# Strassen sums of a SwiGLU feed-forward kept in PSUM, gate and up products interleaved, weight sums formed by accumulating loads

## The chip, the cores and the metric

One core of a Trainium2 chip runs the whole kernel in one launch. The metric is device time in microseconds, and the result is the median of several runs. The engines are TensorE (PE, with its weight loads listed as PEld), VectorE (DVE), ScalarE (ACT), GpSimd (POOL) and SyncE (SP, which here only starts transfers).

## The reference

Two layers of a trunk of width 1024 over 512 latent tokens and 256 context tokens. Each layer is a feed-forward, a mixer of four head groups, and a second feed-forward. The feed-forwards are what the change touches:

```python
def swiglu(h, w_gate, w_up, w_down):
    return (jax.nn.silu(h @ w_gate) * (h @ w_up)) @ w_down

h_lat = h_lat + 0.5 * m_l[2] * swiglu(modulate(rms_norm(h_lat, g_ffn1[l]), m_l[0], m_l[1]),
                                      w1_gate[l], w1_up[l], w1_down[l])
```

All data are fp32, `D_FF` is 2816. Three of the four feed-forwards run over 768 tokens; the last layer's second one runs over the 512 latent tokens alone.

## The kernel before

Every fp32 operand is split into a rounded part `hi` and a rest `lo` (ACT copies `hi` at L143, DVE subtracts at L144), and a matmul of fp32 numbers is three matmuls in PE's float32r format, `lo·hi + hi·lo + hi·hi` (`mm3`, L172). All matmuls of the feed-forward have line L172.

A feed-forward (`ffn`, L504) works through the 2816 hidden channels in six chunks of 4, 2, 4, 4, 4, 4 blocks of 128. The first chunk is done by `first_pairs`. Each of the others is done two blocks at a time by `gate_up` (nine calls in a feed-forward, 36 in the kernel), and then `down` multiplies the chunk's result `g` by `w_down` and adds it to the residual `h` (L306).

`gate_up` computes, for the gate matrix (`m` = 0) and then for the up matrix (`m` = 1), a 2 x 2 block product by Strassen's method in Winograd's form: seven products in place of eight. The weights are four 128 x 512 pieces a11, a12 (first block of channels) and a21, a22 (second block); the tokens are two halves of `hn` columns (384, in the last feed-forward 256), whose seven combinations (B11, B21, T1 and so on) are made once per feed-forward by `token_sums`. One product is four times `mm3`, 12 matmuls of `hn` columns into one PSUM bank. The order of the products is 1, 2, 5, 6, 7, 4, 3. Four of the seven need sums of weights (`ws`, DVE, L454 and L460 in the trace): a21+a22, then minus a11, a11-a21, and a12 minus the second. The products are added to each other by DVE out of PSUM (`tt`, same lines), with one copy by ACT (L478). `ready` takes a finished quarter: SiLU on ACT for the gate (L450), for up the multiplication on DVE and the split into `g`.

`unit` splits a 128 x 512 piece of weights into a pair of tiles from the ring `wr`. That ring has five pairs, and `N_WX` more in a feed-forward: six in all over 768 tokens, ten over 512. A pair comes free when the 12 matmuls that read it are done. `load` takes the next of four `raw` tiles (128 x 1024) in turn and starts the transfer on SP's queue. SP issues in order, and waits in order for tiles to come free.

PSUM has eight banks: six `ps`, and `pone` and `pmod`, which are lent to the feed-forward as banks except where `fills` still needs `pmod` for the modulation vectors (`mod_group`, L189).

The program's order on each engine comes from a list scheduler at compile time. It goes by the order in which the code issues and by a model of durations; `rise(n)` moves what is inside it ahead by `n` places. On the chip each engine runs its list strictly in order.

Of the kernel before, what the change touches and what calls it, by code (L numbers as in the profile page):

```python
# [11 lines left out]
AF = mybir.ActivationFunctionType  # L12
ALU = mybir.AluOpType
AX = mybir.AxisListType

P = 128
# [30 lines left out]
class K:  # L47
# [114 lines left out]
        self.nc.sync.dma_start(r[:parts, :width], src)  # L162
        return r

    def mm3(self, ps, w, x, start, stop):

        (wh, wl), (xh, xl) = w, x
        n = xh.shape[-1]
        for i, (a, b) in enumerate(((wl, xh), (wh, xl), (wh, xh))):
            for c in range(0, n, 512):  # L170
                e = min(n, c + 512)
                self.nc.tensor.matmul(ps[:, c:e], a, b[:, c:e], start=start and i == 0, stop=stop and i == 2)  # L172


    def mod_group(self, l, blocks):
# [132 lines left out]

    def token_operands(self, X, hn, r, gain, l, part, half, kk):

        hi, lo = X[(("B11", "B21"), ("B12", "B22"))[half][kk]]
        for k in range(4):
            s = slice(k * hn, (k + 1) * hn)
            t = self.tmp.popleft()[:, :hn]
            self.modulated(hi[:, s], lo[:, s], t, 4 * kk + k, r, gain, l, part, half * hn, (half + 1) * hn)
            self.tmp.append(t)

    def token_sums(self, X, hn):  # L320

        tt = self.nc.vector.tensor_tensor
        for k in range(4):
            s = slice(k * hn, (k + 1) * hn)
            (b11, c11), (b21, c21), (b12, c12), (b22, c22) = (
                (X[n][0][:, s].bitcast(F32), X[n][1][:, s].bitcast(F32)) for n in ("B11", "B21", "B12", "B22"))
            t, u = (self.tmp.popleft()[:, :hn] for _ in range(2))
            out = lambda n, x: self.split(X[n][0][:, s], X[n][1][:, s], x)
            tt(out=t, in0=b12, in1=b11, op=ALU.subtract)
            tt(out=u, in0=c12, in1=c11, op=ALU.subtract)  # L330
            tt(out=t, in0=t, in1=u, op=ALU.add)
            out("T1", t)
            tt(out=t, in0=b22, in1=t, op=ALU.subtract)
            tt(out=t, in0=t, in1=c22, op=ALU.add)
            out("T2", t)
            tt(out=u, in0=b22, in1=b12, op=ALU.subtract)
            tt(out=t, in0=t, in1=b21, op=ALU.subtract)
            tt(out=t, in0=t, in1=c21, op=ALU.subtract)
            v = self.tmp.popleft()[:, :hn]
            tt(out=v, in0=c22, in1=c12, op=ALU.subtract)  # L340
# [44 lines left out]
    def first_pairs(self, idx, X, g, hn, norm, operands, fills, start):  # L385
# [45 lines left out]
        for f in range(2, 4):  # L431
            self.plain(idx, f, X, g[f], hn, fills)

    def gate_up(self, idx, f, X, g, hn, fills):

        nc = self.nc
        T, SW = self.tmp.popleft, self.sw
        mats = [{}, {}]
        act = {}

        def prod(ps, w, name):
            xh, xl = X[name]
            for k in range(4):
                self.mm3(ps, (w[0][:, k * P:(k + 1) * P], w[1][:, k * P:(k + 1) * P]),
                         (xh[:, k * hn:(k + 1) * hn], xl[:, k * hn:(k + 1) * hn]), k == 0, k == 3)

        def ready(m, i, j, c):

            if m == 0:
                nc.scalar.activation(c, c, AF.Silu)  # L450
                act[i, j] = c
            else:
                t = act[i, j]
                nc.vector.tensor_tensor(out=t, in0=c, in1=t, op=ALU.mult)  # L454
                s = slice(j * hn, (j + 1) * hn)
                self.split(g[i][0][:, s], g[i][1][:, s], t)
                self.tmp.extend((t, c))

        def tt(eng, out, p, q, op):
            eng.tensor_tensor(out=out, in0=p, in1=q, op=op)  # L460
            return out

        def ws(out, p, q, op):
            return tt(vec, out, p, q, op)

        vec = nc.vector
        for m, M in enumerate(mats):
            self.spot(fills)
            for step in (1, 2, 5, 6, 7, 4, 3):
                if step == 1:  # L470
                    M["r"] = [self.load(self.a["w_gu"][idx, f + j, :, m, :], 1024) for j in range(2)]
                (a11, a12), (a21, a22) = ((r[:, :512], r[:, 512:]) for r in M["r"])
                bank = self.banks.popleft()
                ps = bank[:, :hn]
                if step == 1:
                    prod(ps, self.unit(a11), "B11")
                    M["p1"] = T()[:, :hn]
                    nc.scalar.activation(M["p1"], ps, AF.Copy)  # L478
                elif step == 2:
                    prod(ps, self.unit(a12), "B21")  # L480
                    ready(m, 0, 0, tt(vec, T()[:, :hn], M["p1"], ps, ALU.add))
                elif step == 5:
                    M["s"] = ws(SW[0], a21, a22, ALU.add)
                    prod(ps, self.unit(M["s"]), "T1")
                    M["p5"], bank = bank, None
                elif step == 6:
                    prod(ps, self.unit(ws(M["s"], M["s"], a11, ALU.subtract)), "T2")
                    M["u2"] = tt(vec, M["p1"], M["p1"], ps, ALU.add)
                elif step == 7:
                    prod(ps, self.unit(ws(SW[1], a11, a21, ALU.subtract)), "T3")  # L490
                    M["u3"] = tt(vec, T()[:, :hn], M["u2"], ps, ALU.add)
                    tt(vec, M["u2"], M["u2"], M["p5"][:, :hn], ALU.add)
                elif step == 4:
                    prod(ps, self.unit(a22), "T4")
                    ready(m, 1, 0, tt(vec, T()[:, :hn], M["u3"], ps, ALU.subtract))
                    ready(m, 1, 1, tt(vec, M["u3"], M["u3"], M["p5"][:, :hn], ALU.add))
                    self.banks.append(M["p5"])
                elif step == 3:
                    prod(ps, self.unit(ws(M["s"], a12, M["s"], ALU.subtract)), "B22")
                    ready(m, 0, 1, tt(vec, M["u2"], M["u2"], ps, ALU.add))  # L500
                if bank is not None:
                    self.banks.append(bank)

    def ffn(self, l, which, part, n, cuts, fills, start=None):  # L504

# [2 lines left out]
        idx = l * 2 + which  # L508
        hn = n // 2
        with ExitStack() as st:  # L510
            tmp = st.enter_context(self.area("t"))
# [17 lines left out]
            for ci, nf in enumerate(F_CHUNKS):  # L529
# [891 lines left out]
```

## Time and profile before

| what | value |
|---|---|
| median of 3 runs | 2690.11 us (2685.78 to 2691.51) |
| the profiled execution, its own time | 2696.05 us |
| its span from first to last instruction | 2694.2 us |
| PE busy | 2629.0 us (98%), 16021 matmuls |
| DVE busy | 2005.3 us (74%) |
| ACT busy | 1133.1 us (42%) |
| POOL busy | 76.6 us (3%) |
| transfers | 254.15 MB, mean 94 GB/s; every transfer of the program on SP's queue |

Busy is the share of the span in which at least one instruction of the engine was in flight. Matmuls overlap their neighbours, so a matmul's own duration is longer than the time from its start to the next one's start; the latter is what sets the pace.

### The profile page before, as it was taken

To read this page: it belongs to the slowest core of one execution; us is meant where nothing else is said; L and a number is where in the kernel's file an instruction comes from. 1 tells how busy PE (TensorE), PEld (TensorE's weight loads), DVE (VectorE), ACT (ScalarE), POOL (GpSimd) and SP (SyncE) were. 2 spreads that over 40 slices of the span, in tenths; PEclk is the share of its full clock that TensorE was granted. 3 is DMA by queue.
4 is the path that set the end of the run, shared out by engine and by line. 5 is a ranking of instruction groups with operands and counts; after the bars stand their busy time and mean duration, and the time that the engine had idled before them with its cause. 6 is when DMAs were issued, how large, how long until landed. Compare 5 with 4: busy or idle time off the path is not lost.

```text
span 2694.2 us, 40622 instructions
## 1 busy us (share of the span) xinstructions
PE 2629.0 (98%) x16021; PEld 2450.3 (91%) x16021; DVE 2005.3 (74%) x3888; ACT 1133.1 (42%) x2125; POOL 76.6 (3%) x98
## 2 busy tenths in 40 slices
PE   7999999999999999999999999999999999999998
PEld 5999999988887999999999999999998776889998
DVE  5777667679967476767667868677679985788887
ACT  4323323343567342334324523343334576544444
POOL 0000000000212000000000000000000111000000
PEclk9999999999989999999999999999999999999999
DMA  7323223221134342223223112221222133423322
GB/s 257 124 78 119 86 79 110 94 71 50 38 110 145 128 137 96 95 86 118 92 81 122 43 55 63 71 79 56 74 75 80 35 118 119 134 84 103 95 95 79
DMA packets 78272, 254.15 MB, mean 94 GB/s; under 512 B 8704, under 2 KB 14336, under 8 KB 77824
## 3 DMA queue, kind: packets, MB, share of 16 engines
q1 hardware_dynamic: 78080, 251.56, 28.9%
q8 instruction: 125, 2.05, 0.3%
q14 instruction: 67, 0.55, 0.1%
HBM read 249.43 MB, written 2.10 MB: 93 GB/s over the span
## 4 chain that ended last, share of the span: by engine, by line
PE 86%; DVE 8%; ACT 2%; DMA 2%; issue 1%; POOL 0%; SPq 0%; DVEq 0%; ACTq 0%; POOLq 0%
PE ps L172 66%; PE pone L172 8%; PE pmod L172 5%; PE pmod L189 3%; DVE f L631 2%; DMA raw<-in_w_gu 1%; PE ps L606 1%; DVE wl L144 1%; PE pone L770 1%; DVE r L144 1%; PE pone L771 0%; DVE f L144 0%; DMA raw<-in_w_mod 0%; DVE sm L885 0%; DVE sm L833 0%
## 5 line engine op out<-in xcount | busy, mean ns | idle before, releaser
L172 PE MATMUL ps<-x,wh 128*128 128x384 f32 (+1 forms) x3064 | 748.6, 329 | 0.0
L172 PEld LDWEIGHTS ps<-x,wh 128*128 128x128 f32 x3064 | 542.9, 188 | 0.1
L172 PE MATMUL ps<-x,wl 128*128 128x384 f32 (+1 forms) x1532 | 505.1, 330 | 0.0
L143 ACT ACTIVATE wh<-raw 128x512 fp32r<-128x512 f32 (+1 forms) x439 | 275.0, 628 | 435.6 <-PE ps L172 268.5
L144 DVE TENSOR_TENSOR wl<-raw,wh 128x512 fp32r<-128x512 f32 (+1 forms) x439 | 303.1, 692 | 115.7 <-ACT wh L143 113.5
L172 PE MATMUL ps<-t,wh 128*128 128x384 f32 (+2 forms) x1488 | 385.8, 341 | 0.3 <-DVE t L144 0.3
L306 DVE SCALAR_TENSOR_TENSOR h<-ps,hg,h 128x256 f32<-128x256 f32 (+3 forms) x404 | 186.7, 506 | 183.0 <-PE ps L172 182.5
L172 PEld LDWEIGHTS ps<-x,wl 128*128 128x128 f32 x1532 | 287.7, 188 | 7.5 <-issue 3.7
L143 ACT ACTIVATE wh<-t 128x512 fp32r<-128x512 f32 x217 | 136.4, 631 | 337.7 <-PE ps L172 199.6
L172 PEld LDWEIGHTS ps<-t,wh 128*128 128x128 f32 x1488 | 269.2, 188 | 7.1 <-DVE t L144 0.5
L172 PE MATMUL ps<-r,wh 128*128 128x512 f32 (+3 forms) x1070 | 260.9, 335 | 0.6 <-DVE r L301 0.5
L460 DVE TENSOR_TENSOR t<-t,ps 128x384 f32<-128x384 f32 (+1 forms) x422 | 217.6, 521 | 51.7 <-PE ps L172 49.5
L172 PE MATMUL ps<-t,wl 128*128 128x384 f32 (+2 forms) x744 | 253.0, 341 | 2.0 <-ACT t L143 2.0
L143 ACT ACTIVATE t<-t 128x384 fp32r<-128x384 f32 (+2 forms) x247 | 130.7, 537 | 212.3 <-DVE t L454 101.8
L144 DVE TENSOR_TENSOR wl<-t,wh 128x512 fp32r<-128x512 f32 x217 | 149.3, 690 | 92.2 <-ACT wh L143 92.0
L172 PE MATMUL ps<-x,t 128*128 128x384 f32 (+1 forms) x1308 | 204.2, 309 | 0.0
L172 PEld LDWEIGHTS ps<-r,wh 128*128 128x128 f32 (+1 forms) x1070 | 180.3, 188 | 22.3 <-DVE r L301 1.7
L172 PEld LDWEIGHTS ps<-x,t 128*128 128x128 f32 x1308 | 194.1, 188 | 0.0
L172 PE MATMUL ps<-t,t 128*128 128x384 f32 (+2 forms) x948 | 188.1, 345 | 0.0
L172 PEld LDWEIGHTS ps<-t,t 128*128 128x128 f32 x948 | 165.6, 188 | 9.7
L172 PE MATMUL ps<-r,wl 128*128 128x512 f32 (+3 forms) x535 | 170.9, 338 | 2.4 <-ACT r L300 1.8
L144 DVE TENSOR_TENSOR t<-t,t 128x384 fp32r<-128x384 f32 (+2 forms) x247 | 137.8, 570 | 26.4 <-ACT t L143 26.0
(260 smaller groups left out, 4018.1 us busy)
## 6 DMA issues: line engine op xcount, KB each, us to landing
raw<-in_w_gu SPq DMA_DIRECT2D x160, 512.0 KB, 3.8
mraw<-in_w_mod SPq DMA_DIRECT2D x104, 512.0 KB, 4.5
raw<-in_w_dn SPq DMA_DIRECT2D x88, 512.0 KB, 3.7
raw<-in_w_in SPq DMA_DIRECT2D x34, 512.0 KB, 3.5
raw<-in_w_mod SPq DMA_DIRECT2D x24, 512.0 KB, 4.5
raw<-in_w_out SPq DMA_DIRECT2D x20, 512.0 KB, 4.2
i<-in_w_mod SPq DMA_DIRECT2D x32, 256.0 KB, 5.9
raw<-in_w_gu SPq DMA_DIRECT2D x32, 256.0 KB, 3.6
```

The lines of the kernel that those rows point to most:

```text
L143: self.nc.scalar.activation(hi, x, AF.Copy)
L144: self.nc.vector.tensor_tensor(out=lo, in0=x, in1=hi.bitcast(F32), op=ALU.subtract)
L172: self.nc.tensor.matmul(ps[:, c:e], a, b[:, c:e], start=start and i == 0, stop=stop and i == 2)
L189: nc.tensor.matmul(ps[32 * j:32 * j + 32, :256], self.sc[:, k, :], r[:, j * 256:(j + 1) * 256], start=k == 0, stop=k == KD - 1)
L306: nc.vector.scalar_tensor_tensor(out=self.h[:, k, s:e], in0=ps[:, s - a:e - a], scalar=gate[:, k, i:i + 1], in1=self.h[:, k, s:e], op0=ALU ...
L460: eng.tensor_tensor(out=out, in0=p, in1=q, op=op)
L606: self.nc.tensor.transpose(out, in_, self.ident)
L631: nc.vector.scalar_tensor_tensor(out=y[:, :n], in0=u[:, j:j + n], scalar=w[:, j:j + 1], in1=y[:, :n], op0=ALU.mult, op1=ALU.add)
L770: nc.tensor.matmul(po[:, :256], v, p[1], start=start, stop=False)
```

## The change

The four weight sums leave DVE. `added` loads one piece into a tile of the ring `sw` (now six tiles in place of two) by SP and then lets POOL start a second transfer that adds another piece onto it in SBUF. Two sums are made this way at the start (with signs turned so that all are additions); the other two are made from the second by a further accumulating transfer each, in steps 6 and 3, after the tile's split has read it. The signs of the token combinations are turned to match.

The products are no longer added by DVE where PSUM can do it: bank `a` collects products 1, 6, 5 and 3 without being cleared, ACT copying the sum out after 1, 6 and 5 (`kept`); bank `b` holds product 2, then collects 7 and 4. DVE adds only where the two meet.

The order of the products is 1, 2, 7, 6, 5, 3, 4, and each step does gate and up in turn before the next step, so four banks are in use at a time. The number of matmuls is the same.

```diff
+    def added(self, p, q):
+        t = self.turn(self.sw)
+        self.nc.sync.dma_start(t, p)
+        self.nc.gpsimd.dma_start(t, q, accum_op=ALU.add)
+        return t
...
-        for m, M in enumerate(mats):
-            self.spot(fills)
-            for step in (1, 2, 5, 6, 7, 4, 3):
...
+        for step in (1, 2, 7, 6, 5, 3, 4):
+            if step in (1, 5):
+                self.spot(fills)
+            for m, M in enumerate(mats):
+                c = []
                 if step == 1:
-                    M["r"] = [self.load(self.a["w_gu"][idx, f + j, :, m, :], 1024) for j in range(2)]
...
+                    src = [self.a["w_gu"][idx, f + j, :, m, :] for j in range(2)]
+                    r = self.load(src[0], 1024)
+                    M["a11"], M["a12"] = r[:, :512], r[:, 512:]
+                    r = self.turn(self.raw)
+                    nc.sync.dma_start(r[:, 512:], src[1][:, 512:])
+                    M["a22"], M["src"] = r[:, 512:], src
+                    M["s3"] = self.added(src[0][:, :512], src[1][:, :512])
+                    M["s"] = self.added(src[1][:, :512], src[1][:, 512:])
+                    M["a"] = self.banks.popleft()
+                    M["p"] = kept(prod(M["a"], self.unit(M["a11"]), "B11"))
                 elif step == 2:
-                    prod(ps, self.unit(a12), "B21")
-                    ready(m, 0, 0, tt(vec, T()[:, :hn], M["p1"], ps, ALU.add))
+                    M["b"] = self.banks.popleft()
+                    ready(m, 0, 0, tt(M["p"], prod(M["b"], self.unit(M["a12"]), "B21"), M["p"]))
+                    c = [M["p"]]
+                elif step == 7:
+                    M["w"] = prod(M["b"], self.unit(M["s3"]), "T3")
+                elif step == 6:
+                    M["s1"] = self.unit(M["s"])
+                    with self.rise(self.P_UNIT):
+                        nc.gpsimd.dma_start(M["s"], M["src"][0][:, :512], accum_op=ALU.add)
+                    M["u"] = kept(prod(M["a"], self.unit(M["s"]), "T2", False))
                 elif step == 5:
-                    M["s"] = ws(SW[0], a21, a22, ALU.add)
-                    prod(ps, self.unit(M["s"]), "T1")
-                    M["p5"], bank = bank, None
...
+                    M["v"] = kept(prod(M["a"], M["s1"], "T1", False))
+                    ready(m, 1, 1, tt(M["v"], M["w"], M["v"], ALU.subtract))
+                    c = [M["v"]]
+                elif step == 3:
+                    with self.rise(self.P_UNIT):
+                        nc.gpsimd.dma_start(M["s"], M["src"][0][:, 512:], accum_op=ALU.add)
+                    ps = prod(M["a"], self.unit(M["s"]), "B22", False)
+                    ready(m, 0, 1, ps, None if m else T())
+                    self.banks.append(M["a"])
                 elif step == 4:
-                    prod(ps, self.unit(a22), "T4")
-                    ready(m, 1, 0, tt(vec, T()[:, :hn], M["u3"], ps, ALU.subtract))
-                    ready(m, 1, 1, tt(vec, M["u3"], M["u3"], M["p5"][:, :hn], ALU.add))
-                    self.banks.append(M["p5"])
...
+                    ready(m, 1, 0, tt(M["u"], prod(M["b"], self.unit(M["a22"]), "T4", False), M["u"], ALU.subtract))
+                    c = [M["u"]]
+                    self.banks.append(M["b"])
...
-            self.sw = tmp(2, 512)
+            self.sw = tmp(6, 512)
```

Here `prod(..., False)` starts without clearing the bank, and `kept(ps)` is an ACT copy into a tile.

## Rows read from the trace of the kernel before

**Rows 1.** The page: the span, and the chain that ended last by engine.
```profile
span 2694.2 us, 40622 instructions
...
PE 86%; DVE 8%; ACT 2%; DMA 2%; issue 1%; POOL 0%; SPq 0%; DVEq 0%; ACTq 0%; POOLq 0%
```

**Rows 2.** Windows: the four feed-forwards' stretches (first, last, sum); busy us, then clock.
```profile
130.00:575.00 445.00, 445.00 (x2619) 433.64 (x2619) 310.44 (x577) 149.97 (x267) 0.00 (x0) 1.00 0.29 92
...
2350.00:2675.00 325.00, 322.22 (x2245) 301.48 (x2244) 278.17 (x557) 151.59 (x295) 0.00 (x0) 0.99 0.29 93
sum 1645.00, PE 1639.93 PEld 1595.66 DVE 1214.28 ACT 602.68 POOL 0.00; mean PE 409.98 PEld 398.92 DVE 303.57 ACT 150.67 POOL 0.00
```

**Rows 3.** Waits of PE: total us, times, longest.
```profile
PE pone L172 <- ACT t L143: 2.8, 1, 2.8
...
PE ps L172 <- ACT t L143: 2.0, 1, 2.0
...
PE pmod L282 <- DVE acc L256: 1.9, 1, 1.9
...
PE pone L282 <- DVE acc L256: 1.5, 2, 1.3
```

**Rows 4.** Timeline of PE: 12 matmuls of 384 columns, 24 of 256.
```profile
1902.90 2.25 PE L172 MATMUL ps<-t,t 128*128 128x384 f32 x12
1904.98 0.34 PE L172 MATMUL pone<-t,wl 128*128 128x384 f32 x1
...
2410.36 3.00 PE L172 MATMUL ps<-x,t 128*128 128x256 f32 x24
...
2413.20 0.28 PE L172 MATMUL ps<-x,wl 128*128 128x256 f32 x1
```

**Rows 5.** Groups by line and shape: count, busy us, mean ns, idle before.
```profile
L144 DVE TENSOR_TENSOR wl<-raw,wh 128x512 fp32r<-128x512 f32 x435 | 300.5, 693 | 115.4 <-ACT wh L143 113.2
...
L143 ACT ACTIVATE wh<-raw 128x512 fp32r<-128x512 f32 x435 | 273.3, 629 | 434.5 <-PE ps L172 267.4 <-issue 106.6 <-PE pone L172 26.5
...
L460 DVE TENSOR_TENSOR t<-t,ps 128x384 f32<-128x384 f32 x326 | 178.0, 551 | 48.4 <-PE ps L172 47.5
...
L450 ACT ACTIVATE t<-t 128x384 f32<-128x384 f32 x108 | 56.7, 525 | 25.0 <-DVE t L460 24.7
...
L460 DVE TENSOR_TENSOR t<-t,raw 128x512 f32<-128x512 f32 x72 | 49.7, 691 | 2.1
...
L478 ACT ACTIVATE t<-ps 128x384 f32<-128x384 f32 x32 | 15.7, 489 | 37.3 <-PE ps L172 37.3
```

**Rows 6.** Timeline of ACT at the start of one `gate_up`.
```profile
1751.03 0.49 ACT L478 ACTIVATE t<-ps 128x384 f32<-128x384 f32 x1 [1.43 <-PE ps L172]
1751.42 0.62 ACT L143 ACTIVATE wh<-t 128x512 fp32r<-128x512 f32 x1
1753.20 0.63 ACT L143 ACTIVATE wh<-raw 128x512 fp32r<-128x512 f32 x1 [1.16 <-issue]
...
1755.33 0.63 ACT L143 ACTIVATE wh<-raw 128x512 fp32r<-128x512 f32 x1 [0.81 <-PE ps L172]
```

**Rows 7.** Transfers of 256 KB by place: count, KB, median us to landing.
```profile
i<-in_w_mod SPq DMA_DIRECT2D x32, 256.0 KB, 5.9
raw<-in_w_gu SPq DMA_DIRECT2D x32, 256.0 KB, 3.6
...
raw<-in_w_ukv SPq DMA_DIRECT2D x2, 256.0 KB, 3.0
```

**Rows 8.** SP's queue over the first 45 us: packets, MB, share.
```profile
q1 hardware_dynamic: 9024, 15.07, 90.9%
```

**Rows 9.** Time that SP takes to issue one load, ns min/median/max.
```profile
L162 SPq DMA_DIRECT2D raw<-in_w_gu x160: 327/328/1022, 49.3 to 2626.9; - x160
```

**Rows 10.** Timeline of ACT at the end of a feed-forward.
```profile
1472.72 0.63 ACT L143 ACTIVATE x<-raw 128x512 fp32r<-128x512 f32 x1 [3.35 <-DMA raw<-in_w_gu]
1473.25 0.51 ACT L143 ACTIVATE t<-t 128x384 fp32r<-128x384 f32 x1
```

More of the change, by code (lines that the diff above doesn't have):

```diff
@@ L163, in load, with mm3 @@
         return r
-    def mm3(self, ps, w, x, start, stop):
+    def mm3(self, ps, w, x, start, stop, onto=False):
         (wh, wl), (xh, xl) = w, x
@@ L171, in mm3 @@
                 e = min(n, c + 512)
-                self.nc.tensor.matmul(ps[:, c:e], a, b[:, c:e], start=start and i == 0, stop=stop and i == 2)
+                self.nc.tensor.matmul(ps[:, c:e], a, b[:, c:e], start=start and i == 0, stop=stop and i == 2,
+                                      skip_group_check=onto)
     def mod_group(self, l, blocks):
@@ L328, in token_sums @@
             out = lambda n, x: self.split(X[n][0][:, s], X[n][1][:, s], x)
-            tt(out=t, in0=b12, in1=b11, op=ALU.subtract)
-            tt(out=u, in0=c12, in1=c11, op=ALU.subtract)
+            tt(out=t, in0=b11, in1=b12, op=ALU.subtract)
+            tt(out=u, in0=c11, in1=c12, op=ALU.subtract)
             tt(out=t, in0=t, in1=u, op=ALU.add)
             out("T1", t)
-            tt(out=t, in0=b22, in1=t, op=ALU.subtract)
-            tt(out=t, in0=t, in1=c22, op=ALU.add)
+            stt(out=t, in0=t, scalar=-1.0, in1=b22, op0=ALU.mult, op1=ALU.subtract)
+            tt(out=t, in0=t, in1=c22, op=ALU.subtract)
             out("T2", t)
-            tt(out=u, in0=b22, in1=b12, op=ALU.subtract)
-            tt(out=t, in0=t, in1=b21, op=ALU.subtract)
-            tt(out=t, in0=t, in1=c21, op=ALU.subtract)
+            tt(out=u, in0=b12, in1=b22, op=ALU.subtract)
+            tt(out=t, in0=t, in1=b21, op=ALU.add)
+            tt(out=t, in0=t, in1=c21, op=ALU.add)
             v = self.tmp.popleft()[:, :hn]
-            tt(out=v, in0=c22, in1=c12, op=ALU.subtract)
+            tt(out=v, in0=c12, in1=c22, op=ALU.subtract)
             tt(out=u, in0=u, in1=v, op=ALU.add)
@@ L432, in first_pairs, with prod @@
             self.plain(idx, f, X, g[f], hn, fills)
+    def added(self, p, q):
[3 more added lines that the diff above has]
+        return t
     def gate_up(self, idx, f, X, g, hn, fills):
         nc = self.nc
-        T, SW = self.tmp.popleft, self.sw
+        vec, T = nc.vector, lambda: self.tmp.popleft()[:, :hn]
         mats = [{}, {}]
         act = {}
-        def prod(ps, w, name):
+        def prod(bank, w, name, start=True):
@@ L442, in prod @@
             xh, xl = X[name]
             for k in range(4):
-                self.mm3(ps, (w[0][:, k * P:(k + 1) * P], w[1][:, k * P:(k + 1) * P]),
-                         (xh[:, k * hn:(k + 1) * hn], xl[:, k * hn:(k + 1) * hn]), k == 0, k == 3)
-        def ready(m, i, j, c):
+                self.mm3(bank[:, :hn], (w[0][:, k * P:(k + 1) * P], w[1][:, k * P:(k + 1) * P]),
+                         (xh[:, k * hn:(k + 1) * hn], xl[:, k * hn:(k + 1) * hn]), start and k == 0, k == 3, not start)
@@ L449, in ready @@
+            return bank[:, :hn]
+        def ready(m, i, j, c, t=None):
             if m == 0:
-                nc.scalar.activation(c, c, AF.Silu)
-                act[i, j] = c
+                act[i, j] = t = c if t is None else t
+                nc.scalar.activation(t, c, AF.Silu)
             else:
                 t = act[i, j]
-                nc.vector.tensor_tensor(out=t, in0=c, in1=t, op=ALU.mult)
+                vec.tensor_tensor(out=t, in0=c, in1=t, op=ALU.mult)
                 s = slice(j * hn, (j + 1) * hn)
@@ new lines, in ready, with tt, kept @@
+                self.tmp.append(t)
+        def tt(out, p, q, op=ALU.add):
+            vec.tensor_tensor(out=out, in0=p, in1=q, op=op)
+            return out
+        def kept(ps):
+            t = T()
+            nc.scalar.activation(t, ps, AF.Copy)
+            return t
+        for step in (1, 2, 7, 6, 5, 3, 4):
[3 more added lines that the diff above has]
+                c = []
+                if step == 1:
+                    src = [self.a["w_gu"][idx, f + j, :, m, :] for j in range(2)]
[8 more added lines that the diff above has]
+                    M["p"] = kept(prod(M["a"], self.unit(M["a11"]), "B11"))
+                elif step == 2:
+                    M["b"] = self.banks.popleft()
[8 more added lines that the diff above has]
+                    M["u"] = kept(prod(M["a"], self.unit(M["s"]), "T2", False))
+                elif step == 5:
+                    M["v"] = kept(prod(M["a"], M["s1"], "T1", False))
[7 more added lines that the diff above has]
+                    self.banks.append(M["a"])
+                elif step == 4:
+                    ready(m, 1, 0, tt(M["u"], prod(M["b"], self.unit(M["a22"]), "T4", False), M["u"], ALU.subtract))
+                    c = [M["u"]]
+                    self.banks.append(M["b"])
+                if m:
+                    self.tmp.extend(c)
```

27 lines of the change are left out of this document (1 added, 26 removed).

## The prediction

> **What bounds the kernel now.** I read the page first: 86% of the chain that ended last is PE [rows 1]. A mean over the span says nothing of the feed-forward by itself, so the next view is the windows of the four stretches in which `gate_up` and `down` run: PE is busy 1639.93 of 1645 us there, at a granted clock of 1.00, the 2.4 GHz level (0.99 in the last) [rows 2]. DVE, which the change relieves, is at 1214.28 us of the same 1645, and 278.17 of 325 in the last feed-forward. The waits of PE say what the missing 5 us are: 2.8 and 2.0 us, once each, for the split of `g` behind the last product of a chunk [rows 3]. So in the stretches that the change rewrites PE already runs without gaps, and everything DVE does is beside it. PE's pace is 2.08 us for 12 matmuls of 384 columns, and 2.84 us for 24 of 256 [rows 4]. A product therefore takes 2.08 us over 768 tokens (27 calls of `gate_up`, 29 us each) and 1.42 us over 512 (9 calls, 20 us each).
>
> **What the change takes off PE: nothing.** Seven products of 12 matmuls for each matrix stay, with the same shapes. Accumulating onto a bank instead of clearing it changes a flag; the trace has both kinds inside each product (the first of 12 clears, the rest add) at one pace, so I cost it at nothing.
>
> **What it takes off DVE, and adds to ACT.** For each matrix DVE loses four weight sums at 0.69 us and four of seven sums out of PSUM at 0.55 us [rows 5], 4.96 us; over 72 matrices (fewer columns in 18) some 350 us of 2005. PE covers all of it, so it is worth at most the waits behind DVE and ACT, 5 us, and 8 us with the two ends of a feed-forward where PE waits for the sums of squares, 1.9 and 1.5 us [rows 3]. I put the gain at zero: the last product still ends in a DVE sum, a multiplication, a copy by ACT and a split, 0.55 + 0.55 + 0.53 + 0.55 us [rows 5], before `down` can use it. ACT gains two copies out of PSUM for each matrix at 0.49 us [rows 5], 1 us in 15, while it is busy a third of the time [rows 2]. Cost zero as long as the copy gets its turn. The token sums keep their count of instructions; zero.
>
> **Transfers.** Before, a matrix needs two loads of 512 KB. After: one of 512, three of 256 by SP, and four accumulating ones of 256 by POOL, 2.25 MB in place of 1. That is 4.5 MB in 29 us, 155 GB/s, and SP's queue has moved 15.07 MB in 45 us [rows 8], 335 GB/s. An accumulating transfer reads its target too; counted double, 225 GB/s. It fits over 768 tokens. In the last feed-forward it would be 4.5 MB in 20 us, 330 GB/s counted double, at the limit within a pair of calls; `down` between pairs (22 us with little to load) gives it back. SP issues 4 for a matrix in place of 2, at 0.33 us each [rows 9], 1.3 us in 15: zero. SP still waits in order for tiles, and `a22` keeps its `raw` tile until the last step; but six `sw` tiles let the first two sums of the next call start early, and they are used four and more products (8 us) into it, so I cost `added` at zero. POOL does nothing else in these stretches [rows 2]; what queues behind a waiting accumulating load is the next one. The four more `sw` tiles take room that nothing here shows to be missing: zero.
>
> **The links that become late.** Each split needs a free pair in the ring of six. The timeline of ACT shows the rule: a split starts right behind the copy of product 1, then one each 2.1 us, each released by a product that has ended [rows 6]. So a split starts five products ahead of its use, and this is all the cover that an accumulating load in the middle of a call gets. Time from the start of a call, E(k) the end of its product k, from 0, is 2.08(k+1). The order is 1, 1', 2, 2', 7, 7', 6, 6', 5, 5', 3, 3', 4, 4' (the prime is up); the splits go in the same order, with the one of product 5 ahead of the one of product 6.
>
> For up: the split of the second sum (kept for product 5') gets its pair at E(2) = 6.24, and takes 0.63 + 0.69 [rows 5]: 7.56. Only then may POOL add the third piece, L us. Then the split for 6', 1.32 us: 8.88 + L; needed at E(6) = 14.56, so L may be 5.7. Then the second accumulating load, again L, and ACT's copy for the split of 3', at 8.88 + 2L. That copy is not urgent itself. But product 5' adds onto the bank that 6' has just filled, so ACT must first copy that bank out, between E(7) = 16.64 and the start of 5' at E(8) = 18.72. If the split of 3' stands ahead of this copy in ACT's list, the bank is free at 8.88 + 2L + 0.63 + 0.49 = 10.0 + 2L, and PE waits 2L - 8.72 us. For gate the same chain begins two products earlier and is used one earlier: one product more of cover.
>
> Whether it stands ahead is not visible in the old trace; the list is made from modelled durations, and a short modelled L puts it ahead. What speaks for it is the one place where a load was late: ACT stood 3.35 us at a split for a load, the copy of `g` behind it started late [rows 10], and PE's 2.0 us wait [rows 3] is this one. I take it as ahead.
>
> **L.** No accumulating load and no POOL transfer is in the trace. From below it can't beat a plain load of its size, 3.0 us where little else ran [rows 7]: no wait at all. From above, the 5.9 us of a 256 KB load in a queue at 90.9% [rows 7, 8], and the second read of 256 KB at that queue's rate, 0.26 MB at 335 GB/s = 0.8: 6.7 us, a wait of 4.7 us in each call over 768 tokens, 27 x 4.7 = 126 us. Nearest are the loads of these same weights, 3.6 us [rows 7]; with the second read 0.7 to 0.8 and one more issue like SP's 0.33 [rows 9], L = 4.65. The wait is 2 x 4.65 - 8.72 = 0.58 us, over 27 calls 16 us. Over 512 tokens the ring has ten pairs, so the chain begins four products earlier, at -1.42 us; it ends at -1.42 + 1.32 + 4.65 + 1.32 + 4.65 + 1.12 = 11.6 and is needed at 9 x 1.42 = 12.8: zero.
>
> The Trainium skill, DMA: Bandwidth & Descriptors, section Anatomy of one DMA, gives a transfer from POOL as about 2.0 us and its bytes at 436 GB/s, 2.6 us for 256 KB. By that L nothing would be late and the time would not move. The plain loads here already take 3.0 to 5.9 us [rows 7], which disagrees.
>
> **Sum.** The profiled execution's own time is 2696.05 us; PE's work unchanged, +16 us: 2712. That execution is 5.9 us above the median of the runs shown, 2690.11, so the median after is forecast at 2706.
>
> **Rivals.**
>
> *All hidden, no change.* The split of 3' stands behind the copy, or L is under 4.36 us. For it: the plain 3.0 and 3.6 us. Against: two loads in a row, both on the way of in-order ACT. Time 2690, within 5 us.
>
> *Faster by DVE's relief.* The place is the ends of chunks and feed-forwards; DVE's list is shorter, so the last split of `g` and the last sum of squares come earlier. All four waits gone gives 2.8 + 2.0 + 1.9 + 1.5 = 8.2 us, 2682. It decides only if nearly all of them go and no wait comes. Against: the tail of the last product is as long as before.
>
> *One bank for four products.* PE waits for the copy even with no load late. Each of three copies in a call has one product of cover, 2.08 us; two splits, a SiLU and the copy ahead of it would be 0.63 + 0.63 + 0.53 + 0.49 = 2.28, 0.2 too much. In 3 x 27 places it is 16 us, and with 1.42 us of cover and some 2.0 us of work 3 x 9 x 0.6 = 16 us more: 2722. Against: ACT is idle two thirds of the time [rows 2] and starts such a copy at once [rows 6]. The Trainium skill, Perfetto Trace Analysis, section Matmuls, asks for just the opposite of this change: independent groups should rotate through banks, so that the evacuation of one overlaps the next. The old kernel does so, and PE has no wait of this kind in its rows, so the trace agrees as far as it goes.
>
> *Accumulating loads much slower than plain ones.* L of 6.7 us or more, by POOL's work on each or by adding at a lower rate than copying, and transfers then saturate in the last feed-forward: 2690 + 126 and more, 2816.
>
> **How the numbers follow.** The forecast, a late chain that costs 5 to 75 us, 0.46. No change 0.25. Faster 0.12. The bank 0.05. Slow loads 0.12. The forecast's own range is 2695 to 2765; taking in the rival on the other side, 2682 to 2765 leaves out the slow loads and a little below. What a measurement of this kernel can tell from no change is about 0.2%, 5.4 us. Faster by that needs nearly all of the 8.2 us: 0.11. Within it: the unchanged case and the mild end of the forecast, 0.28. Slower 0.61.
>
> **What would show it.** DVE some 350 us less busy, ACT some 70 more, 16021 matmuls as before at the same 2.08 us for a product. Waits of PE in the `gate_up` stretches over 768 tokens, once a call, at the first matmul of product 5', released by an ACT copy that stood behind a split waiting for a POOL transfer; none in the last feed-forward. Accumulating loads landing in 4 to 5.5 us. If PE stays without gaps, the step on ACT's order or on L is wrong; if the waits stand at product 6, L is over 5.7; if they are at product 7 or in `down`, I have overlooked a link.

## The result, and the profile after

The median rose from 2688.54 to 2888.43 us, a ratio of 1.0748 with a 95% interval of 1.0726 to 1.0769. I had forecast 2706, and a range up to 2765: the direction was right, the size was not. Where do the 190.7 us by which the profiled span grew lie?

The page of the kernel after, its span, its engines and its two DMA queues (q1 is SP's, q0 POOL's), answers to [rows 1, 8]:

```profile
span 2884.9 us, 41270 instructions
...
PE 2684.1 (93%) x16021; PEld 2487.0 (86%) x16021; DVE 1719.1 (60%) x3312; ACT 1171.0 (41%) x2269; POOL 327.8 (11%) x386
...
q1 hardware_dynamic: 98816, 270.44, 28.8%
q0 software_dynamic: 41472, 75.52, 16.2%
```

The matmuls are the same 16021. PE is idle 200.8 us (2884.9 - 2684.1) where it was idle 65.2: 135.6 of the 190.7. The other 55.1 are busy time, which grew from 2629.0 without one matmul more. The windows of the four feed-forwards, first, last and sum, answer to [rows 2]:

```profile
130.00:640.00 510.00, 478.98 (x2743) 457.75 (x2742) 254.99 (x471) 173.80 (x326) 57.90 (x72) 0.98 0.49 124
...
2510.00:2860.00 350.00, 307.49 (x2000) 283.46 (x2000) 189.10 (x347) 141.09 (x296) 57.64 (x66) 0.94 0.58 136
sum 1850.00, PE 1715.94 PEld 1642.93 DVE 942.35 ACT 654.10 POOL 236.11; mean PE 428.99 PEld 410.73 DVE 235.59 ACT 163.53 POOL 59.03
```

Where PE ran without gaps it is now idle 134 of 1850 us, and the granted clock is lower, above all in the last feed-forward. The waits of PE say for what (total us, times, longest):

```profile
PE ps L172 <- DVE t L471: 59.3, 27, 5.6
PE ps L172 <- ACT t L476: 45.9, 21, 4.0
PE pmod L172 <- DVE t L471: 10.8, 6, 2.8
...
PE pone L172 <- DVE t L471: 10.0, 5, 7.0
```

L476 is `kept`, ACT's copy out of a bank; L471 is `tt`, DVE's sum that reads a bank. PE waits to add onto a bank that an engine has still to read. But these reads take half a microsecond; it is what stands ahead of them that is late. The waits of ACT, same columns:

```profile
ACT wh L143 <- DMA t<-in_w_gu: 202.3, 87, 6.9
ACT t L143 <- DMA t<-in_w_gu: 104.1, 40, 10.3
```

306 us in which ACT stands at a split for a tile of `sw`. In the four stretches of the kernel before, ACT waited for loads 6.6 us in all, in four places, of which [rows 10] shows one.

**Which product waits.** One call has 168 matmuls with the token operand `x`, 12 to a product, so PE's idle time before the first matmul of each can be added up by product. I do this for every kernel below (us; "768" are the 27 calls over 768 tokens, "last" the nine over 512):

| kernel | 768: before 7' | 768: before 5 | 768: other | last | lost inside products |
|---|---|---|---|---|---|
| before | 0 | 0 | 0 | 0 | 17 |
| after | 38.8 | 44.7 | 1.0 | 42.5 | 65 |

"Lost inside" is what the matmuls of these products took, from the start of the first to the start of the last, above eleven twelfths of a product by the pace of [rows 4]. The two sums, 127 of waits and 48 of pace (65 - 17), are 175 of the 190.7 us. Of the other 16, some 11 are the last matmul before each wait, which nothing overlaps: with it, the matmuls with `x` are busy 59 us longer (988.4 to 1047.4). So product 5', where I had put the wait, does not wait over 768 tokens; 5 and 7' do, and products in the last feed-forward too. Three places show how.

**Product 5.** The timeline of the kernel after, in one call (start, us, engine, line; in brackets the idle time before, and what ended it):

```profile
1390.25 0.86 POOL L512 DMA_DIRECT2D t<-in_w_gu  x1 [1.72 <-DVE wl L144]
1394.91 0.86 POOL L512 DMA_DIRECT2D t<-in_w_gu  x1 [3.80 <-DVE wl L144]
1395.19 0.63 ACT L143 ACTIVATE wh<-t 128x512 fp32r<-128x512 f32 x1 [1.41 <-DMA t<-in_w_gu]
1399.89 0.63 ACT L143 ACTIVATE t<-t 128x512 fp32r<-128x512 f32 x1 [4.07 <-DMA t<-in_w_gu]
1400.42 0.47 ACT L476 ACTIVATE t<-ps 128x384 f32<-128x384 f32 x1
1400.95 0.69 PE L172 MATMUL ps<-x,wl 128*128 128x384 f32 x1 [3.97 <-ACT t L476]
```

L512 are the second accumulating loads of the call, for steps 3 and 3'. ACT splits their tiles at 1395.19 and 1399.89, as soon as each has landed; only then comes the copy of product **6**, for which PE waits 3.97 us. Both splits stand ahead of the copy of the gate product, one product earlier than I had placed it. ACT's list has this order in all 27 calls over 768 tokens; 19 of them wait before 5, 2.35 us each on average.

**Product 7'.** The same view, in another call:

```profile
1891.60 0.86 POOL L441 DMA_DIRECT2D t<-in_w_gu  x1 [1.00 <-DMA t<-in_w_gu]
1892.21 1.17 POOL L504 DMA_DIRECT2D t<-in_w_gu  x1
1899.07 0.63 ACT L143 ACTIVATE wh<-t 128x512 fp32r<-128x512 f32 x1 [5.24 <-DMA t<-in_w_gu]
1899.73 0.69 DVE L144 TENSOR_TENSOR wl<-t,wh 128x512 fp32r<-128x512 f32 x1 [5.61 <-ACT wh L143]
1900.34 0.55 DVE L471 TENSOR_TENSOR t<-ps,t 128x384 f32<-128x384 f32 x1
1900.95 0.69 PE L172 MATMUL ps<-x,wl 128*128 128x384 f32 x1 [4.07 <-DVE t L471]
```

L441 is the accumulating load of a first sum, L504 the one for step 6. POOL issues in order: L504 goes out at 1892.21, behind first sums that had waited for SP's loads. Its tile is split at 1899.07 by ACT and at 1899.73 by DVE, and behind that stands DVE's sum of 2', which reads the bank onto which 7' is to add. The prediction had DVE with nothing late in its list. This call is one of seven in which the load for step 6 goes out 1.5 to 1.9 us after the split that frees its tile (0.4 in the other 20) and takes 6.6 to 7.2 us. These seven have 27.5 of the 38.8 us before 7', and no wait before 5.

**The last feed-forward.** The ring has ten pairs here, and I had costed it at zero for that reason:

```profile
2575.36 0.88 POOL L512 DMA_DIRECT2D t<-in_w_gu  x1 [7.62 <-DVE t L144]
2575.98 1.15 POOL L504 DMA_DIRECT2D t<-in_w_gu  x1
2580.32 0.63 ACT L143 ACTIVATE t<-t 128x512 fp32r<-128x512 f32 x1 [5.30 <-DMA t<-in_w_gu]
2581.52 0.63 ACT L143 ACTIVATE t<-t 128x512 fp32r<-128x512 f32 x1 [0.57 <-DMA t<-in_w_gu]
2582.79 0.42 DVE L471 TENSOR_TENSOR t<-pone,t 128x256 f32<-128x256 f32 x1
2583.26 0.58 PE L172 MATMUL pone<-x,wl 128*128 128x256 f32 x1 [6.99 <-DVE t L471]
```

The splits have moved ahead in the lists: those for steps 3 and 6' now stand ahead of DVE's sum of product **2**, and 7 waits 6.99 us. This is the longest wait of the nine calls. In the other eight the splits for 6 and 6' stand ahead of the sum of 2, and that for 3 ahead of the sum of 2'. Of the 42.5 us, 25.5 stand before 7 and 15.8 before 7'.

**The clock.** Windows of the kernel after around the wait at 1397 to 1401 (columns as in [rows 2]; the clock is third from the end):

```profile
1390.00:1396.00 6.00, 5.73 (x33) 5.62 (x33) 2.27 (x5) 1.79 (x3) 1.73 (x2) 1.00 0.57 89
...
1401.00:1404.00 3.00, 3.00 (x10) 3.00 (x11) 1.62 (x3) 1.31 (x3) 0.69 (x1) 0.50 0.37 83
```

Before the wait the granted clock is 1.00, the 2.4 GHz level; after 3.97 us without work it is 0.50, the 1.2 GHz level, and 10 matmuls fill 3 us. So a wait can cost more than its length, and this is most of the busy time that grew: all 37 products that took over 0.5 us too long are among the first four behind a wait. Not every wait does it; 29 of the 61 before products have such a product among the next two.

### The profile page after: what moved, and what is told of

Its sections match the earlier page's. It is cut to its first block, busy times and chain, and to the rows that moved or that the text cites. A ratio compares the mean times of both kernels' runs of the same rounds, so it can differ in the third digit from the quotient of the medians.

```text
span 2884.9 us, 41270 instructions
## 1 busy us (share of the span) xinstructions
PE 2684.1 (93%) x16021; PEld 2487.0 (86%) x16021; DVE 1719.1 (60%) x3312; ACT 1171.0 (41%) x2269; POOL 327.8 (11%) x386
## 2 busy tenths in 40 slices
DMA packets 140484, 348.59 MB, mean 121 GB/s; under 512 B 15616, under 2 KB 21248, under 8 KB 140032
## 3 DMA queue, kind: packets, MB, share of 16 engines
HBM read 343.80 MB, written 2.10 MB: 120 GB/s over the span
## 5 line engine op out<-in xcount | busy, mean ns | idle before, releaser
L172 PE MATMUL ps<-x,wh 128*128 128x384 f32 (+1 forms) x3224 | 814.2, 338 | 0.0
L172 PE MATMUL ps<-x,wl 128*128 128x384 f32 (+1 forms) x1612 | 551.4, 342 | 84.8 <-ACT t L476 45.9
L172 PEld LDWEIGHTS ps<-x,wh 128*128 128x128 f32 x3224 | 593.8, 195 | 0.1
L143 ACT ACTIVATE wh<-raw 128x512 fp32r<-128x512 f32 x448 | 279.1, 626 | 475.7 <-PE ps L172 357.9
L172 PEld LDWEIGHTS ps<-x,wl 128*128 128x128 f32 x1612 | 314.4, 195 | 107.1 <-ACT t L476 55.3
L144 DVE TENSOR_TENSOR wl<-raw,wh 128x512 fp32r<-128x512 f32 x448 | 309.1, 692 | 163.3 <-ACT wh L143 153.4
L307 DVE SCALAR_TENSOR_TENSOR h<-ps,hg,h 128x384 f32<-128x384 f32 (+3 forms) x400 | 185.0, 507 | 226.0 <-PE ps L172 225.3
L441 POOL DMA_DIRECT2D t<-in_w_gu x144 | 126.4, 889 | 1614.8 <-DMA t<-in_w_gu 1558.1
L144 DVE TENSOR_TENSOR wl<-t,wh 128x512 fp32r<-128x512 f32 x208 | 143.9, 692 | 265.1 <-ACT wh L143 262.1
L143 ACT ACTIVATE wh<-t 128x512 fp32r<-128x512 f32 x208 | 131.1, 630 | 386.0 <-DMA t<-in_w_gu 202.3
L143 ACT ACTIVATE t<-t 128x384 fp32r<-128x384 f32 (+2 forms) x256 | 136.2, 536 | 262.8 <-DMA t<-in_w_gu 104.1
L144 DVE TENSOR_TENSOR t<-t,t 128x384 fp32r<-128x384 f32 (+2 forms) x256 | 146.3, 575 | 148.8 <-ACT t L143 148.2
L172 PE MATMUL ps<-x,t 128*128 128x256 f32 (+1 forms) x1332 | 213.6, 315 | 21.5 <-DVE t L471 21.3
```

The source lines that it names most:

```text
L143: self.nc.scalar.activation(hi, x, AF.Copy)
L144: self.nc.vector.tensor_tensor(out=lo, in0=x, in1=hi.bitcast(F32), op=ALU.subtract)
L307: nc.vector.scalar_tensor_tensor(out=self.h[:, k, s:e], in0=ps[:, s - a:e - a], scalar=gate[:, k, i:i + 1], in1=self.h[:, k, s:e], op0=ALU ...
L441: self.nc.gpsimd.dma_start(t, q, accum_op=ALU.add)
```

## The experiments

The theory after the result, **the list**: loads of POOL that land late hold the in-order lists of ACT and DVE at splits, and the reads of PSUM behind them are what PE waits for. Rivals: **the banks** (adding in PSUM ties a product to the reading of the last one, and this costs by itself), and **bytes** (348.59 MB in place of 254.15, transfers too many).

### e1: the weight sums back on DVE, sums in PSUM and order of products as after

```diff
-                    M["s3"] = self.added(src[0][:, :512], src[1][:, :512])
-                    M["s"] = self.added(src[1][:, :512], src[1][:, 512:])
...
-                        nc.gpsimd.dma_start(M["s"], M["src"][0][:, :512], accum_op=ALU.add)
+                    tt(M["s"], M["s"], M["a11"])
```

SP loads both pieces of the weights again; the kernel has two more `raw` tiles than the one after, and two `sw` tiles as before.

> The changed kernel with the four weight sums of a matrix back on DVE and both weight pieces loaded by SP, and two more raw tiles; sums in PSUM, order of products and interleaving stay. Theory of the list (ACT and DVE stand in order at splits that wait for POOL's loads, and the copies out of PSUM stand behind them): no load is waited for in the middle of a call, the waits of PE before products 5 and 7' go, 2675 to 2705 us. Theory of the banks (four products onto one bank leave too little time to read it, whatever the loads do): waits stay, over 2850. Theory of the bytes (94 MB more traffic is what costs): as the list, 2675 to 2705, since the traffic is gone too.

Measured: 2687.16 us, ratio 0.9996 (0.9982 to 1.0009). The page:

```profile
PE 2623.6 (98%) x16021; PEld 2445.8 (91%) x16021; DVE 1886.3 (70%) x3600; ACT 1183.8 (44%) x2269; POOL 76.3 (3%) x98
```

No wait before any product over 768 tokens. The order of the products and the adding in PSUM cost nothing, and DVE's 119 us less (2005.3 to 1886.3) give nothing. The banks fall: the whole loss came with the loads, by their place or by their bytes, which e1 takes out together.

### e4: no accumulating load in the middle of a call; e8: only that for step 6; e9: only that for step 3

```diff
-                    with self.rise(self.P_UNIT):
-                        nc.gpsimd.dma_start(M["s"], M["src"][0][:, :512], accum_op=ALU.add)
...
-                    with self.rise(self.P_UNIT):
-                        nc.gpsimd.dma_start(M["s"], M["src"][0][:, 512:], accum_op=ALU.add)
```

e4 leaves both out, e8 the second, e9 the first.

> The changed kernel without the two accumulating loads in the middle of a call (steps 6 and 3), so that products 6 and 3 use the first sum; the two sums at the start stay accumulating loads. Theory of the list: the chain of two loads that holds the copies before 5 is gone, and the split that holds DVE before 7 and 7' too; what is left is late first sums, 2690 to 2750 us. Theory of the banks: over 2850. Theory of the bytes: 38 of 94 MB gone, about 2810.

> The changed kernel with one of the two accumulating loads in the middle of a call, that of step 6; product 3 uses the sum as product 6 left it. Theory of the list: DVE's reads of banks 2 and 2' still stand behind the split for product 6, so the waits before 7 and 7' stay (80 us and the lower clock behind them); ACT's copy of 6 no longer stands behind a late split for 3, so the waits before 5 go (45 us): 2800 to 2840 us. If each load in the middle of a call costs the same by itself: half way between 2699 and 2888, 2794 us, with half of each wait.

> The changed kernel with one of the two accumulating loads in the middle of a call, that of step 3; product 6 uses the first sum. Theory of the list: the load is issued one L earlier, so the split for 3 is done about when the copy of 6 is due, the waits before 5 shrink under 0.5 us in a call, those before 7 and 7' go: 2700 to 2720 us. If each load in the middle of a call costs the same by itself: 2794 us.

| kernel | us | ratio (95%) | 768: 7' | 768: 5 | 768: other | last |
|---|---|---|---|---|---|---|
| e4, none | 2699.48 | 1.0044 (1.0028 to 1.0060) | 0 | 0 | 0 | 3.4 |
| e9, step 3 | 2727.99 | 1.0133 (1.0103 to 1.0162) | 0 | 0.5 | 0 | 20.5 |
| e8, step 6 | 2791.13 | 1.0367 (1.0337 to 1.0397) | 35.3 | 0 | 1.2 | 29.4 |
| after, both | 2888.43 | 1.0748 (1.0726 to 1.0769) | 38.8 | 44.7 | 1.0 | 42.5 |

The 144 first sums still come by POOL in e4, and cost some 12 us with it (0.44%). The waits before 7' belong to the load for step 6. Those before 5 belong to neither alone: of these kernels, only the one with the chain of two has them. e8 and e9 cost 92 and 29 us over e4, together 120; both loads cost 189. e9 came out 8 us over what I expected, with 20.5 us of waits in the last feed-forward. e8's time is under the list theory's 2800 to 2840 and 3 us from the 2794 that equal halves gave, so by itself it speaks for the rival. e9's, 66 us under the same 2794, refutes equal halves, and so do the waits: e8 has 35.3 us before 7' and none before 5, not half of each.

### e5: the first sums without POOL

```diff
-        self.nc.gpsimd.dma_start(t, q, accum_op=ALU.add)
```

> The changed kernel with the two sums at the start of a call replaced by a single SP load each (the second pieces left out), so that POOL only issues the two accumulating loads in the middle of a call. Theory of the list: waits before 5 and 7 stay, but POOL's queue is free and step 6's load lands in about 4.2 us instead of 5.1, 1 us earlier and without POOL's own delay of up to 2 us: 2760 to 2830 us. If the late first sums are what is late: as the run without the loads in the middle, under 2710 us.

Measured: 2813.70 us, 1.0451 (1.0421 to 1.0481). PE's waits, and POOL's loads (count, KB, median us to landing):

```profile
PE ps L172 <- ACT t L475: 58.9, 29, 3.1
PE ps L172 <- DVE t L470: 16.9, 13, 3.4
```

```profile
t<-in_w_gu POOLq DMA_DIRECT2D x144, 256.0 KB, 4.1
```

L475 is `kept` here, L470 `tt`. By product: 0.8 before 7', 57.1 before 5, 28.1 in the last. The waits before 7' have gone: they came from the first sums' loads, with which step 6's goes out later and takes longer (median 5.1 us in the kernel after, 4.0 here). Whether it is the queue or the shared traffic that lengthens it, e5 doesn't tell. Those before 5 stay, though a load takes 4.1 us, less than the 4.36 from which my formula starts. By place it fits: the copy of 6 is wanted one product, 2.08 us, before that of 6', so the wait is 2L - 6.64. With medians of 4.0 for step 6 and 4.2 for step 3 that is 1.56 us a call, 42 in all, and 57.1 were measured (2.1 a call). The formula leaves out that POOL starts each of the two loads 0.4 us after the split that frees its tile has ended; with 0.8 us for that it gives 2.36.

e5 also settles the bytes. The traffic of two kernels, the first row e4's and the second e5's:

```profile
DMA packets 119745, 310.80 MB, mean 115 GB/s; under 512 B 13312, under 2 KB 18944, under 8 KB 119296
```

```profile
DMA packets 119747, 310.82 MB, mean 111 GB/s; under 512 B 13312, under 2 KB 18944, under 8 KB 119296
```

Both have 144 accumulating loads. With those at the start of a call the time is 2699.48 us, with those in the middle 2813.70: the place costs, not the amount.

### e3: POOL's loads plain, without adding

```diff
-                        nc.gpsimd.dma_start(M["s"], M["src"][0][:, :512], accum_op=ALU.add)
+                        nc.gpsimd.dma_start(M["s"], M["src"][0][:, :512])
```

and the same for the other three sums.

> The changed kernel with POOL's transfers plain in place of accumulating, so that each sum is left at its last piece alone; the same transfers, waits and order. If adding in the transfer is what is slow, L falls from 5.0 us to about 4.2, and as PE's wait before 5 goes with two L and that before 7' with one, some 1 to 1.6 us in a call: 2830 to 2855 us. If POOL's issue and the landing are slow by themselves, L stays within 0.3 us of 5.0 and the time within 15 us of 2888. Theory of the bytes: the second read of the target is gone, under 2800.

Measured: 2768.30 us, 1.0301 (1.0270 to 1.0332). POOL's loads here, for the row after it of the kernel after:

```profile
t<-in_w_gu POOLq DMA_DIRECT2D x288, 256.0 KB, 3.6
```

```profile
t<-in_w_gu POOLq DMA_DIRECT2D x288, 256.0 KB, 5.0
```

Same reads from memory (343.80 MB), same number of loads, same order in the lists of ACT and DVE: 1.4 us less for each load takes 120 us off the time, twice what I expected at most. A microsecond of a load in the middle counts twice, since two stand in a chain, and then again by the clock. By product: 7.3 before 7', 20.6 before 5, 22.7 in the last. With 3.4 and 3.4 us the corrected formula gives 0.2 us a call, and 0.96 with the 0.8 us of the issues; 0.76 were measured. The time is also where the bytes theory had put it, under 2800, since the second read of the target is gone; e3 does not tell the two apart, e4 and e5 do.

### e6: the reads ahead of the splits

```diff
+                    with behind(last["sum"]):
+                        w6 = self.unit(M["s"])
...
+                    with behind(last["copy6"]):
+                        w3 = self.unit(M["s"])
```

Here `behind` makes the list place the split for 6 after DVE's sum of 2', and that for 3 after ACT's copy of 6'.

> The changed kernel with two places fixed by hand in the engines' lists: the split for product 6 stands behind DVE's sum of 2', and the split for product 3 behind ACT's copy of 6'. Loads, sums and products are as in the change. Theory of the list: the waits before 5, 7 and 7' (127 us with what the lower clock costs behind them, 182 in all) mostly go; a later split can hold PE before 6 and 3 instead, under 2 us in a call; 2700 to 2770 us. Theory of the banks: the reads already come as early as the banks allow, little change, over 2850. Theory of the bytes: same traffic, over 2850.

Measured: 2802.78 us, 1.0429 (1.0391 to 1.0467), 33 us over what I expected at most. Over 768 tokens it did what the theory says: the waits before 7' and 5 are gone, and 24.9 us in place of 84.5 are left, before 6, 6' and 3, where PE now waits for a split itself. In the last feed-forward 52.4 us stay (16.0 before 7, 7.1 before 7', 29.4 before 3), and this is where the expectation failed. With the reads first the loads are still late, only for something else.

### e2 and e11: the old order and the old sums out of PSUM, with accumulating loads

e2 has all four sums by loads; e11 leaves the two in the middle out.

```diff
+        for m, M in enumerate(mats):
+            self.spot(fills)
+            for step in (1, 2, 5, 6, 7, 4, 3):
...
-                        nc.gpsimd.dma_start(M["s"], src[0][:, :512], accum_op=ALU.add)
...
-                        nc.gpsimd.dma_start(M["s"], src[0][:, 512:], accum_op=ALU.add)
```

The added lines are those of e2, the removed ones those that e11 leaves out of it.

> The old order of products, gate before up, DVE adding the products out of six to eight banks in turn, but with the four weight sums by accumulating loads as in the change, so the same transfers. Theory of the list: a late split still holds ACT and DVE, but no product waits for the read of a bank that was filled one product before, and within one matrix the loads have 2 to 3 products more of cover: 2690 to 2740 us. If the loads are late for the splits themselves, whatever the banks: over 2800 us. Theory of the bytes: about 2880, since the traffic is that of the change.

> The old order of products and the old sums by DVE out of PSUM, with the first two sums of a matrix by accumulating loads, and the two loads in the middle left out (so steps 6 and 3 multiply by the second sum as it stands; the output is not the reference's). With all four by loads this was 2909. The list theory, if it holds for this order too: the loss lies at the middle loads, whatever stands behind the splits that wait for them: 2690 to 2720. If in this order the first sums are late already (gate's step 5 is the third product, and up's start sums stand behind gate's middle loads on POOL): 2750 or more.

Measured: e2 2908.76 us, 1.0804 (1.0773 to 1.0836); e11 2696.72 us, 1.0030 (1.0017 to 1.0044). e2 refutes a part of the list theory as I had put it: I thought that without shared banks a late split would be covered, and it is as slow as the change. Its waits of PE:

```profile
PE ps L172 <- DVE wl L144: 36.4, 15, 8.3
PE ps L172 <- ACT t L143: 28.4, 13, 3.3
PE ps L172 <- DVE t L144: 24.3, 17, 6.9
PE pmod L197 <- ACT t L195: 22.2, 3, 10.6
```

PE waits for the splits of the sums themselves (the L144 rows, but 4.4 us) and for the split of `g` before `down` (the L143 row) and the modulation vectors' copy, which stand in the same lists. In this order 6 follows directly on 5, from whose split on its tile may be added to, with no product of the other matrix in between. Its time is nearest to the 2880 of the bytes theory. But e11, which keeps half of POOL's loads, loses 8 us and not half: again the middle loads are nearly all of it, 212 of e2's 220 us.

### e7: the first sums by loads, the middle ones by DVE

```diff
-                    with self.rise(self.P_UNIT):
-                        nc.gpsimd.dma_start(M["s"], M["src"][0][:, :512], accum_op=ALU.add)
+                    tt(M["s"], M["s"], M["a11"])
```

and so for `a12`.

> The two first sums of a matrix stay accumulating loads by POOL; the two sums in the middle of a call are made by DVE again, in the same tile, from the pieces that stand in the raw tiles. All else is as after the change. The list theory (ACT and DVE stand in order at splits that wait for the loads of the middle of a call): no wait of PE over 768 tokens, 0 to 10 us in the last feed-forward, 2692 to 2702 us, as with the middle loads left out (2699). If it was the amount of loads that POOL issues and the bytes, half of each is gone: about 2790. It can't be better than with all four sums on DVE (2687).

Measured: 2700.03 us, 1.0051 (1.0036 to 1.0066): no wait over 768 tokens, 5.8 us in the last. The middle sums cost nothing as an instruction of DVE, which waits for no transfer. It is 13 us over e1, so loads buy nothing for the first sums either.

### e10: the sum for step 6 made at the start

```diff
+                    M["s6"] = self.added(src[1][:, :512], src[1][:, 512:], src[0][:, :512])
...
-                        nc.gpsimd.dma_start(M["s"], M["src"][0][:, :512], accum_op=ALU.add)
-                    M["u"] = kept(prod(M["a"], self.unit(M["s"]), "T2", False))
+                    M["u"] = kept(prod(M["a"], self.unit(M["s6"]), "T2", False))
...
-                        nc.gpsimd.dma_start(M["s"], M["src"][0][:, 512:], accum_op=ALU.add)
+                        nc.gpsimd.dma_start(M["s6"], M["src"][0][:, 512:], accum_op=ALU.add)
```

> The sum for step 6 is made at the start of the call in a tile of its own (a plain load and two accumulating ones), and only the sum for step 3 is still a load in the middle, onto that tile. Loads of a matrix rise from 2.25 to 2.75 MB, POOL's from four to five. The list theory: the chain of two loads in the middle is gone, the waits before 5 go, and those before 7' go with the load of step 6, unless the longer start sums hold POOL's queue; 2720 to 2790. If bytes or the number of POOL's loads set the loss: 2900 or more, above the 2888 of the change.

Measured: 2845.68 us, 1.0596 (1.0578 to 1.0613), above my range and below that of bytes. The waits before 7' are gone, as expected; before 5 41.6 us stay, and the last feed-forward has 57.0. POOL's own rows say why, its waits first, then its timeline:

```profile
POOL t L442 <- issue: 42.9, 35, 4.2
POOL t L512 <- issue: 39.6, 19, 4.1
```

```profile
1393.28 0.87 POOL L442 DMA_DIRECT2D t<-in_w_gu  x1 [2.30 <-DMA t<-in_w_gu]
1393.91 1.14 POOL L512 DMA_DIRECT2D t<-in_w_gu  x1
1396.02 0.89 POOL L442 DMA_DIRECT2D t<-in_w_gu  x1 [0.97 <-issue]
1400.28 0.87 POOL L512 DMA_DIRECT2D t<-in_w_gu  x1 [3.37 <-issue]
```

82.5 us, before 54 loads, in which POOL stood at a load and the profile shows nothing that it waited for. The load issued at 1393.28 landed at 1399.97, 0.31 us before the one at 1400.28 went out; that one is the load for 3', and ACT's split of it, and the copy of 6 behind it, came 4.5 us later. So a longer queue of sums at the start puts off the one load in the middle. Bytes as such do not explain it: with more of them than in the kernel after, the time is less.

## Why the prediction was wrong

**PE without gaps, DVE's relief worth nothing, the banks' cost nothing: right.** e1 has the banks, and 119 us of DVE's relief, at 0.9996; e4 has all the relief (DVE busy 1721.3 us) and is no faster, 1.0044. DVE's instructions took 349 us less, as forecast (350); its busy time fell only by 286, since they overlap. ACT's copies cost 65 us (98.2 - 33.4), as forecast (70); its busy time rose by 38. The Trainium skill, Perfetto Trace Analysis, section Matmuls, would have banks rotate; e1 keeps them tied and loses nothing, as long as nothing late stands ahead of the reads.

**L: nearly right.** I took 4.65 us, and 4 to 5.5 to be seen; the median is 5.0. In the middle of a call it is 5.1 for step 6 and 4.2 for step 3, 9.3 us for the chain, as I had it (2 x 4.65). By the Trainium skill, DMA: Bandwidth & Descriptors, section Anatomy of one DMA, a transfer of POOL's of 256 KB would take 2.6 us, an estimate from its 2.0 us and 436 GB/s; the runs have medians of 3.6 for a plain load of POOL's and 4.1 to 6.0 for an adding one, so they disagree.

**The step that failed: the place of the late split.** The prediction had the split of 3' ahead of ACT's copy of 6', one product too late. It stands ahead of the copy of 6, and "2L - 8.72" should have been 2L - 6.64: 2.66 us with my own L, 72 us over 27 calls in place of 16. Measured are 44.7 us before 5, 2.35 a call in the 19 calls that wait there; the seven in which PE has already lost 3.5 to 4.3 us before 7' have no wait before 5. e5, whose L is below my break-even and which yet waits 2.1 us a call, shows the place; e9 and e8 show that it takes both loads.

**A link overlooked: DVE.** I followed ACT's list alone. Each split has a half on DVE, and DVE's sum of 2', or 2 in the last feed-forward, stands behind it. In seven calls the load for step 6 goes out late behind the first sums, since POOL issues in order: "what queues behind a waiting accumulating load is the next one" was written down, and costed at nothing. 38.8 us, 27.5 of them in these seven; e5 takes them away. The prediction's own sign of an overlooked link, waits at product 7, came in the last feed-forward.

**The last feed-forward at zero.** "the ring has ten pairs, so the chain begins four products earlier" is true of the room, but the splits then move ahead of the reads in the lists too. 42.5 us. That the ten pairs cause it is argued from the timeline; no run changed their number.

**A term left out: the clock.** I counted a wait at its length. After the wait of 3.97 us PE went on at the 1.2 GHz level; over all products this is 48 us.

These are 44.7 + 38.8 + 42.5 + 48 and 1.0, 175 us, and 186 with the last matmuls before the waits, against 16 in the sum. "Slow loads", the rival that came nearest (2816), had the wrong reason: the loads are as fast as I had thought.

The loss lies in the two loads in the middle of a call, by e1, e4, e5 and e11, and its size follows L, by e3. Open are the last 5 us, e4's and e7's 12 to 13 us over e1, and what POOL waits for at an issue in e10. No version was faster than the kernel before; e1 equals it.

## What to carry to other kernels

Where PE has no gaps, an operation of DVE that is ready on time costs nothing, and a transfer in its place can only be late. Before a dependent load goes into the middle of a pipeline, ask of every in-order engine that reads its result, ACT and DVE alike, what stands behind the read, and of the issuing queue what stands ahead of it; two such loads in a chain count twice. A late split costs whatever comes next in the list, so moving one victim out of the way (e6) or removing the bank conflict (e2) only finds the next.

## What the runs showed of the hardware

An accumulating load of 256 KB from POOL lands in a median of 5.0 us, a plain one in 3.6. Issuing it keeps POOL busy 0.87 to 0.92 us, a plain one 0.54:

```profile
L504 POOL DMA_DIRECT2D t<-in_w_gu x72 | 66.5, 924 | 107.0 <-DVE wl L144 80.8 <-DVE t L144 7.8 <-DVE t L465 7.3
```

```profile
L504 POOL DMA_DIRECT2D t<-in_w_gu x72 | 38.8, 538 | 125.6 <-DVE wl L144 93.4 <-DMA t<-in_w_gu 18.2 <-DVE t L465 7.7
```

The first row is the kernel after, the second e3, from the groups by line.

A load that waits for a split goes out 0.40 us after the split has ended (median of the 27 calls, the kernel after and e5).

In no run were more than three accumulating loads under way. In e10, 51 of the 54 loads before which POOL stood without a named wait found two others under way as they went out, and 45 of these followed within 0.5 us of a landing. Four plain ones were under way four times in e3. That the queue takes no fourth fits this, but was not tested by itself.
